# Weight sums of a down-projection made by accumulating DMAs instead of VectorE

## The chip, the core and the metric

The kernel runs on one core of a Trainium2 chip. The metric is the device time of one execution in microseconds (us); the kernel before takes 1341.7 us (median of three runs, 1338.76 to 1344.27). The core's engines work at the same time, each through its own list of instructions in order, and wait for one another by semaphores: TensorE (PE) does the matmuls, VectorE (DVE) and ScalarE (ACT) the elementwise work, GpSimd (POOL) small things, and SyncE (SP) issues nearly all transfers (DMAs). A DMA issued from any of them is carried out by the core's 16 DMA engines.

## The reference, cut to what matters

Two decoder layers over 512 positions of width 1024. Each layer has a token mixer (attention beside a gated delta rule) and then a channel mixer, in which the change lies:

```python
def conv_glu_ffn(h, ffn_w_in, ffn_conv_w, ffn_conv_b, ffn_w_out):
    u = causal_dwconv(h @ ffn_w_in, ffn_conv_w) + ffn_conv_b
    gate, up = jnp.split(u, 2, axis=-1)
    return (jax.nn.gelu(gate, approximate=True) * up) @ ffn_w_out
...
for l in range(DEPTH):              # DEPTH = 2
    ...
    h = rms_norm(x, norm_pre_ffn[l])
    f = conv_glu_ffn(h, ffn_w_in[l], ffn_conv_w[l], ffn_conv_b[l], ffn_w_out[l])
    x = x + rms_norm(f, norm_post_ffn[l]).astype(x.dtype)
```

`ffn_w_in` is 1024 x 5632, `ffn_w_out` (the down-projection) 2816 x 1024, all float32.

## The kernel before, in words

**Precision.** Each float32 operand of a large matmul is split into a high part, rounded by ACT to the PE's format (`wh`, `hh`), and a remainder, formed by DVE (`wl`, `hl`); a product is three matmuls (`three`).

**Up-projection** (`chan_proj`, called with `glu`). The 5632 columns are taken 128 at a time: 44 *weight tiles* of 1024 x 128 (512 KB), each giving 24 matmuls of 512 columns. Each tile goes through `load_w`: an SP load into `st` (three buffers), ACT's cast into `wh` (three buffers), DVE's remainder into `wl` (three). A load therefore waits on SP until DVE has finished with the tile three back, and a cast waits until PE has finished with the tile three back. The first four tiles (`early`) are done in two halves and kept in other buffers. Tiles alternate: a gate tile and an up tile make one *block* `jb` of 128 hidden channels, so there are 22 blocks of two tiles. After each tile `glu` applies the convolution (ACT, then two DVE operations, `fgu`) and after the second one the GELU and the product, which is `hid[jb]` (`g`).

**Down-projection** (`products`). It is a 2 x 2 block product done with seven multiplications instead of eight. The weight is cut in four quarters, W00, W01, W10, W11 (first index: half of the 2816 rows; second: half of the 1024 columns). Three products use quarters as they are; four use sums: U1 = W00 + W01, T3 = W01 + W11, T2 = W00 + T3, T4 = W10 + T2. Each quarter has 11 pieces of 128 rows.

**The sums** (`weight_sums`, line 855). They are made during the up-projection, a piece `k` at a time. At the blocks listed in `SUMS_AT` (line 32) the four 128 x 512 pieces of 256 KB are loaded into `ws` buffers. At the next block `sums.pop(0)()` (line 893) runs `add`: four in-place additions on DVE, in an order in which the second overwrites an operand of the first, the third reads the first's result and overwrites an operand of the second, and the fourth reads the third's result. Then SP stores the four results into DRAM tensors (`wsum`; the profile drops digits, so U1 is `U` there, and T2, T3 and T4 are `T`), from which `products` loads them much later.

**What sets the order.** A scheduler places the instructions of each engine by the priorities given in `prio` and by its own estimate of durations; once placed, the order on an engine is fixed. SP in particular works through one list: a store whose data is not ready holds up every load behind it.

Of the kernel before, what the change touches and what calls it, by code (L numbers as in the profile page):

```python
# [13 lines left out]
OP = mybir.AluOpType  # L14
# [14 lines left out]
NF = 22  # L29
EPS = 1e-6  # L30
NB = 32
SUMS_AT = (0, 2, 3, 5, 7, 8, 10, 12, 13, 15, 17)


class Engines:
# [51 lines left out]
def hybrid_trunk(ctx: ExitStack, tc: tile.TileContext, a, out):  # L87
    nc = Engines(tc)
# [43 lines left out]
    def big(name, dtype=F32, shape=(P, T), tag="b2", bufs=None):  # L132
        return bp.tile(list(shape), dtype, name=name, tag=tag, bufs=bufs)
# [7 lines left out]
    def pair(name, shape=(P, 2, T)):  # L141
        return big(name, F32, shape, "b4", 2)
# [202 lines left out]
    for l in range(NL):  # L345
# [500 lines left out]
        hid, accs, xf = [], {}, {}  # L846
# [3 lines left out]
        def w_f2(kh, s, k, n=1):  # L850
            return a["w_f2"][l, kh, s][:, k:k + n, :]

        sums = []

        def weight_sums(k):

            w = {}
            for kh in range(2):
                for s in range(2):
                    w[kh, s] = big("ws")  # L860
                    nc.sync.dma_start(w[kh, s].unsqueeze(1), w_f2(kh, s, k))

            def add():
                for o, i in (((1, 1), (0, 1)), ((0, 1), (0, 0)), ((0, 0), (1, 1)), ((1, 0), (0, 0))):
                    nc.vector.tensor_tensor(w[o], w[o], w[i], op=OP.add)
                for v, o in zip(wsum, ((0, 1), (1, 1), (0, 0), (1, 0))):
                    nc.sync.dma_start(v[:, k, :], w[o])

            sums.append(add)

        def operand(p, k, src):
            xf[p, k] = big("xf", F32R, (P, 2, T // 2))
            split(xf[p, k][:, 0, :], xf[p, k][:, 1, :], src)
# [3 lines left out]
        def glu(b, ps):  # L877
            jb, g = b // 2, b % 2
            cb = jb + g * NF
            if g == 0:  # L880
                accs[jb] = pair("fgu")
            acc = accs[jb][:, g, :]
            nc.scalar.activation(acc, ps, AF.Identity, scale=fw[:, l, cb, 2:3], bias=fb[:, l, cb:cb + 1])
            for j in range(1, 3):
                nc.vector.scalar_tensor_tensor(acc[:, j:], ps[:, :T - j], fw[:, l, cb, 2 - j:3 - j], acc[:, j:],
                                               op0=OP.mult, op1=OP.add)
            if g == 1:
                ga = accs[jb][:, 0, :]
                nc.scalar.activation(ga, ga, AF.Gelu_apprx_tanh)
                hid.append(big("g"))  # L890
                nc.vector.tensor_tensor(hid[jb], ga, acc, op=OP.mult)
                if sums:
                    sums.pop(0)()
                if jb in SUMS_AT:
                    weight_sums(SUMS_AT.index(jb))
                if jb >= half:
                    k = jb - half
                    x1, x2 = hid[k], hid[jb]
                    operand("X11", k, x1[:, r1])
                    nc.vector.tensor_tensor(x1[:, r1], x1[:, r1], x1[:, r2], op=OP.subtract)  # L900
                    nc.vector.tensor_tensor(x1[:, r2], x1[:, r2], x2[:, r2], op=OP.subtract)
                    operand("D", k, x1[:, r2])

        with prio(L + 7):
            run(chan_proj(lambda b: a["w_f1"][l, b // 2 + NF * (b % 2)], 2 * NF, 4, glu, turns))
# [185 lines left out]
```

## Time and profile before

| | |
|---|---|
| time, median of 3 | 1341.7 us (1338.76 to 1344.27) |
| profiled execution, its own time | 1343.61 us |
| its span, first to last instruction | 1341.7 us |
| PE busy | 1304.3 us (97%) |
| DVE busy | 1009.1 us (75%) |
| ACT busy | 725.3 us (54%) |
| POOL busy | 187.3 us (14%) |
| the additions on DVE (`ws<-ws`), both layers | 60.7 us, 88 operations |
| moved by DMA | 193.14 MB, mean 144 GB/s |

The up-projection of the first layer runs from about 333 to 566 us of the span, that of the second from about 994 to 1228 us. In the rows of a timeline or of the chain of waits the first column is the start and the second the length, in us; in rows of groups "x44" is a count, followed by busy time and mean ns of one, and after the second bar by the idle time of the engine just before them and what ended it; in a table by stretches each engine has busy us and its number of instructions, then come the clock that TensorE was granted, the mean busy share of the 16 DMA engines, and the rate. "PE pm" is a matmul into one of the large accumulators.

### The profile page before, as it was taken

Reading aid. Unit: us, or ns where it says so; the run is one execution under the profiler, and the core shown is the slowest. Engines: PE = TensorE matmul, PEld = TensorE weight load, DVE = VectorE, ACT = ScalarE, POOL = GpSimd, SP = SyncE. Lnnn points to the kernel's source line nnn. Section 1 sums busy time; section 2 is a strip of 40 time slices with the busy share of each in tenths; the row PEclk is TensorE's granted clock in tenths of the full one; section 3 lists DMA queues with packets and bytes.
Section 4 is the critical chain, followed back from the end, with each engine's and each line's share of the span. In section 5 each row is a group of like instructions: output and inputs, shape, how many; then the busy total and the mean of one; then the engine's idle time right before and its main releaser. Section 6 shows DMA issues by size and latency. Waiting matters only on the chain.

```text
span 1341.7 us, 19369 instructions
## 1 busy us (share of the span) xinstructions
PE 1304.3 (97%) x6892; PEld 1083.4 (81%) x6892; DVE 1009.1 (75%) x1956; ACT 725.3 (54%) x1458; POOL 187.3 (14%) x246
## 2 busy tenths in 40 slices
PE   8999999999999999999999999998999999999997
PEld 6787877878888888888777877877888888888876
DVE  6656888868576788798777568888667767888885
ACT  5635966665333444467546369666543334444673
POOL 0019421111000000030010293102010000001201
PEclk9999999999999999999999999999999999999999
DMA  6233211243466566366642422104335566653665
GB/s 227 92 106 95 71 53 36 82 144 131 136 230 219 188 219 212 110 179 185 218 164 72 124 82 73 52 19 134 118 126 188 191 224 198 222 187 105 201 184 162
DMA packets 75489, 193.14 MB, mean 144 GB/s; under 512 B 13409, under 2 KB 13953, under 8 KB 75394
## 3 DMA queue, kind: packets, MB, share of 16 engines
q1 hardware_dynamic: 74882, 190.87, 44.4%
q0 software_dynamic: 512, 1.05, 0.4%
q8 instruction: 54, 0.88, 0.3%
q14 instruction: 41, 0.34, 0.1%
HBM read 161.99 MB, written 29.90 MB: 143 GB/s over the span
## 4 chain that ended last, share of the span: by engine, by line
PE 80%; DVE 8%; ACT 6%; POOL 2%; DMA 2%; issue 2%; SPq 0%; POOLq 0%; DVEq 0%; ACTq 0%
PE pm L54 67%; PE pw L54 13%; DVE wl L54 2%; ACT junk L54 1%; DVE xs L54 1%; ACT wh L54 1%; DVE x L54 1%; ACT sc L54 1%; POOL nr L54 1%; DVE hl L54 1%; DVE xf L54 1%; DMA st<-in_w_f 1%; ACT Vt L54 0%; POOL pr L54 0%; POOL qs L54 0%
## 5 line engine op out<-in xcount | busy, mean ns | idle before, releaser
L54 DVE TENSOR_TENSOR wl<-st,wh 128x1024 fp32r<-128x1024 f32 (+1 forms) x250 | 282.7, 1136 | 163.1 <-ACT wh L54 161.0
L54 PE MATMUL pm<-hh,wh 128*128 128x512 f32 (+1 forms) x1024 | 373.6, 367 | 3.9 <-ACT hh L54 3.9
L54 ACT ACTIVATE wh<-st 128x1024 fp32r<-128x1024 f32 (+1 forms) x254 | 245.8, 972 | 242.3 <-PE pm L54 223.4
L54 PE MATMUL pm<-hl,wh 128*128 128x512 f32 (+1 forms) x1024 | 375.2, 368 | 0.0
L54 PE MATMUL pm<-hh,wl 128*128 128x512 f32 (+1 forms) x1024 | 374.0, 367 | 1.1 <-DVE wl L54 1.1
L54 PEld LDWEIGHTS pm<-hh,wh 128*128 128x128 f32 x1024 | 194.8, 191 | 34.6 <-ACT hh L54 5.2
L54 PEld LDWEIGHTS pm<-hh,wl 128*128 128x128 f32 x1024 | 195.1, 191 | 30.4 <-DVE wl L54 1.3
L54 PEld LDWEIGHTS pm<-hl,wh 128*128 128x128 f32 x1024 | 195.3, 192 | 29.0
L54 PE MATMUL pm<-wh,xf 128*128 128x512 f32 x528 | 164.5, 391 | 0.0
L54 PE MATMUL pm<-wh,hh 128*128 128x512 f32 x384 | 154.4, 405 | 0.0
L54 PE MATMUL pm<-wh,hl 128*128 128x512 f32 x384 | 153.1, 399 | 0.0
L54 PE MATMUL pm<-wl,hh 128*128 128x512 f32 x384 | 151.2, 395 | 0.8 <-DVE wl L54 0.8
L54 DVE SCALAR_TENSOR_TENSOR fgu<-pm,fw,fgu 128x511 f32<-128x511 f32 (+1 forms) x176 | 131.1, 745 | 21.9 <-ACT fgu L54 19.9
L54 PEld LDWEIGHTS pm<-wh,xf 128*128 128x128 f32 x528 | 99.1, 188 | 21.2 <-ACT e L54 0.6
L54 PE MATMUL pm<-wl,xf 128*128 128x512 f32 x264 | 103.6, 392 | 0.5 <-DVE wl L54 0.5
L54 POOL TENSOR_TENSOR g<-g 128x256 f32<-128x256 f32 x22 | 25.4, 1174 | 493.1 <-DVE xf L54 493.1
L54 PEld LDWEIGHTS pm<-wl,hh 128*128 128x128 f32 x384 | 72.4, 189 | 14.8 <-DVE wl L54 2.0
L54 PEld LDWEIGHTS pm<-wh,hl 128*128 128x128 f32 x384 | 72.4, 188 | 14.2
L54 PEld LDWEIGHTS pm<-wh,hh 128*128 128x128 f32 x384 | 72.1, 189 | 14.0 <-ACT wh L54 0.5
L54 ACT ACTIVATE sc<-sc,mx 128x128 f32<-128x128 f32 (+3 forms) x128 | 69.5, 558 | 22.2 <-DVE mx L54 21.6
L54 ACT ACTIVATE fgu<-pm,fb,fw 128x512 f32<-128x512 f32 x88 | 66.9, 761 | 18.6 <-PE pm L54 18.6
L54 ACT ACTIVATE fgu<-fgu 128x512 f32<-128x512 f32 x44 | 27.8, 632 | 90.8 <-DVE fgu L54 90.7
(228 smaller groups left out, 1801.5 us busy)
## 6 DMA issues: line engine op xcount, KB each, us to landing
st<-in_w_f SPq DMA_DIRECT2D x118, 512.0 KB, 3.7
ws<-in_w_f SPq DMA_DIRECT2D x88, 256.0 KB, 4.7
T<-ws SPq DMA_DIRECT2D x66, 256.0 KB, 2.3
st<-in_w_at SPq DMA_DIRECT2D x32, 512.0 KB, 3.7
st<-T SPq DMA_DIRECT2D x30, 512.0 KB, 4.0
st<-in_w_dn SPq DMA_DIRECT2D x24, 512.0 KB, 3.8
st<-in_w_out SPq DMA_DIRECT2D x16, 512.0 KB, 3.6
U<-ws SPq DMA_DIRECT2D x22, 256.0 KB, 2.0
```

The source lines that it names most:

```text
L54: r = f(*args, **kwargs)
```

## The change

The four additions are no longer DVE operations. Each is a DMA issued from POOL that reads one `ws` buffer and accumulates into another, both in SBUF (`accum_op=OP.add`). The stores stay on SP, but are put one block after the additions: a list of (block, action) replaces the list of actions. Two entries of `SUMS_AT` move, 3 to 4 and 12 to 11, so that in the order of blocks the pieces come alone at 0 and 2, in neighbouring pairs at (4, 5), (7, 8), (10, 11), and alone at 13, 15, 17. A store now waits for an accumulating DMA where it waited for DVE.

```diff
-SUMS_AT = (0, 2, 3, 5, 7, 8, 10, 12, 13, 15, 17)
+SUMS_AT = (0, 2, 4, 5, 7, 8, 10, 11, 13, 15, 17)
...
             def add():
                 for o, i in (((1, 1), (0, 1)), ((0, 1), (0, 0)), ((0, 0), (1, 1)), ((1, 0), (0, 0))):
-                    nc.vector.tensor_tensor(w[o], w[o], w[i], op=OP.add)
+                    nc.gpsimd.dma_start(w[o], w[i], accum_op=OP.add)
+
+            def store():
                 for v, o in zip(wsum, ((0, 1), (1, 1), (0, 0), (1, 0))):
                     nc.sync.dma_start(v[:, k, :], w[o])
 
-            sums.append(add)
+            sums.append((len(hid), add))
+            sums.append((len(hid) + 1, store))
...
-                if sums:
-                    sums.pop(0)()
+                while sums and sums[0][0] < len(hid):
+                    sums.pop(0)[1]()
```

On SP, from the first pieces of the first layer on, the list of transfers was this (`st<-in_w_f` loads a weight tile, `ws<-in_w_f` the four pieces; T_3578 is T3, U_3577 is U1, T_3579 is T2, T_3580 is T4):

```order
L54 DMA st<-in_w_f 128x1024 x10
L54 DMA ws<-in_w_f 128x512 x4
L54 DMA T_3578<-ws 128x512
L54 DMA U_3577<-ws 128x512
L54 DMA T_3579<-ws 128x512
L54 DMA T_3580<-ws 128x512
L54 DMA st<-in_w_f 128x1024 x2
L54 DMA ws<-in_w_f 128x512 x4
```

In the changed kernel, at the same place for a pair of pieces (blocks 4 and 5), it is this:

```order
L54 DMA ws<-in_w_f 128x512 x4
L54 DMA st<-in_w_f 128x1024
L54 DMA T_3578<-ws 128x512
L54 DMA st<-in_w_f 128x1024
L54 DMA ws<-in_w_f 128x512 x4
L54 DMA U_3577<-ws 128x512
L54 DMA T_3579<-ws 128x512
L54 DMA st<-in_w_f 128x1024
L54 DMA T_3580<-ws 128x512
L54 DMA T_3578<-ws 128x512
L54 DMA st<-in_w_f 128x1024
L54 DMA U_3577<-ws 128x512
```

The four stores of a piece, which stood together, are now spread, with loads of weight tiles (and of the next pieces) queued behind each of them. For a lone piece the list is the pieces' load, a tile, T3, a tile, U1 and T2, a tile, T4, a tile, and then the next pieces' load.

On POOL, with the semaphores each waits for, the accumulating DMAs of the first two pieces of the first layer stand like this (DMASW0 to DMASW7 are the semaphores of the DMAs that POOL issues, DMAHW those of SP's):

```order
L54 DMA ws<-ws 128x512 [waits DMAHW7_49,DMAHW5_49,PE_49]
L54 DMA ws<-ws 128x512 [waits DMAHW4_49,DMASW0_49]
L54 DMA ws<-ws 128x512 [waits DMASW1_49,PE_49]
L54 DMA ws<-ws 128x512 [waits DMAHW6_49,DMASW2_49]
L54 DMA ws<-ws 128x512 [waits DMAHW7_49,DMAHW1_49,PE_49]
L54 DMA ws<-ws 128x512 [waits DMAHW6_49,DMASW4_49]
L54 DMA ws<-ws 128x512 [waits DMASW5_49]
```

POOL had nothing at this place before. Now 44 DMAs per layer stand there, and the second, third and fourth of each piece wait for the one ahead of them; the first of a piece waits for its loads alone.

## The prediction

> **What bounds the kernel now.** I first read the chain of waits through the up-projection, where every changed instruction lies. For the two layers it is one piece each (start, length):
>
> ```profile
> 332.56 278.21 PE pm L54 x1289
> 994.40 278.22 PE pm L54 x1289
> ```
>
> For 278 us TensorE never waits for anything. The table by stretches, over the 44 weight tiles alone, says the same: PE is busy in all of its 233.4 us at full clock, POOL does nothing, and the DMA engines are busy 58% of the time.
>
> ```profile
> 332.60:566.00 233.40, 233.40 (x1093) 195.98 (x1092) 169.06 (x243) 92.54 (x127) 0.00 (x0) 1.00 0.58 191
> ```
>
> So DVE, at 169 of 233 us, sets nothing here. The pace is ACT's evacuation of one tile after another (`fgu<-pm`), which PE releases; the two rows of `wh` are casts of later tiles:
>
> ```profile
> 365.40 0.76 ACT L54 ACTIVATE fgu<-pm,fb,fw 128x512 f32<-128x512 f32 x1
> ...
> 369.87 1.06 ACT L54 ACTIVATE wh<-st 128x1024 fp32r<-128x1024 f32 x1 [0.95 <-PE pm L54]
> 370.84 0.76 ACT L54 ACTIVATE fgu<-pm,fb,fw 128x512 f32<-128x512 f32 x1
> ```
>
> 370.84 - 365.40 = 5.44 us for a tile, 10.9 us for a block of two.
>
> What else could stop PE is SP's list. It is read in time order, together with DVE's addition:
>
> ```profile
> 298.09 35.21 SPq L54 DMA_DIRECT2D st<-in_w_f  x10
> 333.35 1.86 SPq L54 DMA_DIRECT2D ws<-in_w_f  x4
> 352.08 0.33 SPq L54 DMA_DIRECT2D T<-ws  x1
> ...
> 355.90 5.77 SPq L54 DMA_DIRECT2D st<-in_w_f  x2
> 361.71 2.46 SPq L54 DMA_DIRECT2D ws<-in_w_f  x4
> ```
> ```profile
> 368.73 2.87 DVE L54 TENSOR_TENSOR ws<-ws 128x512 f32<-128x512 f32 x4 [0.54 <-DMA ws<-in_w_f]
> 371.52 1.22 DVE L54 TENSOR_TENSOR wl<-st,wh 128x1024 fp32r<-128x1024 f32 x1
> ```
>
> Already now SP stands still at a store for 17 us (335.2 to 352.1), and PE doesn't notice. How long may it? The eleventh tile (ten were loaded ahead) is issued at 355.90. PE needs it when ten tiles are through, and this row of groups, over 339 to 382 us, counts ten evacuations, of which the last is the row behind it:
>
> ```profile
> L54 ACT ACTIVATE fgu<-pm,fb,fw 128x512 f32<-128x512 f32 x10 | 7.7, 765 | 9.3 <-PE pm L54 9.3
> ```
> ```profile
> 381.72 0.76 ACT L54 ACTIVATE fgu<-pm,fb,fw 128x512 f32<-128x512 f32 x1
> ```
>
> Before 381.7 come the load (3.7 us to landing, the row below), the cast 1.06 and the remainder 1.22, with some 0.2 between: 6.2 us. So a tile's load may be late by 381.7 - 6.2 - 355.9 = **19.6 us** before PE waits.
>
> ```profile
> st<-in_w_f SPq DMA_DIRECT2D x118, 512.0 KB, 3.7
> ws<-in_w_f SPq DMA_DIRECT2D x88, 256.0 KB, 4.7
> ```
>
> **The change, part by part.** *Removed:* 44 additions per layer from DVE, 60.7 us in both:
>
> ```profile
> L54 DVE TENSOR_TENSOR ws<-ws 128x512 f32<-128x512 f32 x88 | 60.7, 689 | 8.4 <-DMA ws<-in_w_f 6.4
> ```
>
> Worth on the path: nothing, since no PE instruction there waited for DVE. In the whole program the waits of matmuls and of weight loads for `wl` are
>
> ```profile
> PE pm L54 <- DVE wl L54: 2.3, 5, 1.1
> PEld pm L54 <- DVE wl L54: 5.7, 12, 1.3
> ```
>
> 8.0 us, which is the most that a freer DVE could give back; since the two chains above hold none of them, I take 0. The order of ACT's and DVE's other work also shifts a little at the same spots; 169 - 44 x 0.69 = 139 us of DVE work hides under 233 us of PE, so 0 as well.
>
> *Added:* 88 accumulating DMAs from POOL. POOL has nothing else there (it sat idle for 244 us before its next operation, which comes after the last tile), so its issue time costs nothing by itself:
>
> ```profile
> 574.45 2.61 POOL L54 TENSOR_TENSOR g<-g 128x256 f32<-128x256 f32 x3 [244.12 <-DVE xf L54]
> ```
>
> What costs is that in each piece's four DMAs each waits for the one ahead, and that SP's stores, with tile loads behind them, wait for those. Call L the time from the issue of one accumulating DMA to that of the next one that waits for it. The trace has no accumulating DMA. Its nearest row is a 64 KB copy that POOL issues, with the POOL operation that waits for it:
>
> ```profile
> 189.33 0.57 POOL L54 DMA_DIRECT2D zc<-dX  x1 [3.07 <-PE pw L54]
> 191.59 1.53 POOL L54 COPY zt<-zc 32x128 f32<-32x128 f32 x2 [1.69 <-DMA zc<-dX]
> ```
>
> 191.59 - 189.33 = 2.26 us. That is the lower bound of L (a quarter of the bytes, nothing added). The upper bound is the longest landing of any of these 256 KB transfers, 6.9 us:
>
> ```profile
> DMA to landing us min/median/max: 2.0/3.6/6.9
> ```
>
> Between them: all 16 engines at work move 191 / 0.58 = 329 GB/s, so 256 KB take 0.80 us and 64 KB 0.20. An accumulation reads both its source and its destination, two passes: L = 2.26 - 0.20 + 2 x 0.80 = 3.66 us with free engines. They aren't always free: SP issues a tile (512 KB, 1.6 us of all engines) right behind T3's and T2's stores, that is, as the second and the fourth DMA begin; at worst each costs a full 1.6, which is +0.8 on the mean, so 4.5. I take 3.9, nearer the free end, because a tile's load begins some time after its issue and overlaps only partly.
>
> The Trainium skill, "DMA: Bandwidth & Descriptors", section "Anatomy of one DMA — SWDGE (gpsimd) path", puts a POOL-issued DMA at 2.0 us plus its bytes at 436 GB/s. For 64 KB that is 2.15 against the measured 2.26; for two passes of 256 KB it gives an estimated 3.2 instead of my 3.66 to 4.5. By it the margin below would be 0.9 us, not 0.2; I keep the rate of this stage's own row.
>
> *Moved, and the tipping point.* A lone piece must get through SP in 2 blocks, 21.8 us. From the last of its four loads (issued at 361.71 + 2.46 - 0.37 = 363.8) to the first addition (368.73) are 4.9 us; then four links; then T4's store, a tile and the four loads of the next piece, 0.3 + 0.4 + 1.9 = 2.6: together 7.5 + 4L. A pair has 3 blocks, 32.6 us, and the second piece's chain begins when POOL has issued the first's fourth DMA (0.6 us): 4.9 + 3L + 0.6 + 4L + 2.6 = 8.1 + 7L. Between blocks 2 and 17 lie three lone pieces and three pairs, so the lateness that builds up in a layer is 3 (4L - 14.3) + 3 (7L - 24.5) = 33L - 116 us. The first 19.6 are free: PE loses 33L - 136 per layer, **66L - 272** in both, from L = 4.1 us on. At 3.9 the lateness is 13 us a layer, hidden under the tiles loaded ahead: 0.
>
> *Traffic.* In 233.4 us the engines are busy 0.58 x 233.4 = 135; 44 accumulations of two passes add 44 x 1.6 = 70, together 205 of 233: it fits.
>
> Sum: 0 - 0 + 0 on the profiled execution's 1343.6 us (span 1341.7, and 1.9 around it). The median of the runs shown is 1.9 us below that execution, so I predict 1342 for the median.
>
> **The rivals.**
>
> *The chain paces SP (slower).* If L is over 4.1 us, stores hold the tile loads back until PE starves, at each of the later pieces. For it: the margin is 0.2 us on a price that no row shows, and each further 0.1 us costs 6.6. Against it: only L decides, and 3.66 is what free engines give. At L = 4.8 it costs 66 x 4.8 - 272 = 45: 1387 us; at the upper bound of 6.9, 183: 1525.
>
> *The DMA engines are full.* If an accumulation takes three passes (two reads and a write apart), 44 x 2.4 = 106, and 135 + 106 = 241 us of work in 233: +8 a layer, some 1357 us. Against it: copies read and write in one pass at the rate above.
>
> *POOL is held up while it issues.* POOL's issue may be slowed by DVE. At worst each waits for one DVE operation of 1.22 us: L = 3.9 + 1.2 = 5.1, 66 x 5.1 - 272 = 65, 1407 us. The issue row above took 0.57 with DVE busy in the same slices, which speaks against it. The Trainium skill, "SBUF — State Buffer", section "Who interferes with whom", has such a rule: DMAs issued by GpSimd can be starved by DVE operations that take the port pair both share. It names copies and tensor_scalar, not the two-input operations that fill this stage; no row here shows such a stall.
>
> *A freer DVE helps after all.* All 8.0 us of waits for `wl` vanish: 1334. Against it: they lie outside the stage.
>
> **How the numbers follow.** What a measurement can tell from no change is about 0.5%, 6.7 us. No change, 1342 us: 0.55. The chain paces SP: 0.32. Engines full: 0.06. POOL held up: 0.03. Faster: 0.04. So faster 0.04, same 0.55, slower 0.41. Alone, the no-change case would range from 1337 to 1348. For 8 in 10 I go up to L = 4.9 (66 x 4.9 - 272 = 51, 1393), which leaves about a third of the chain rival and half of POOL's above, some 0.14, and down to 1336, which leaves 0.03: 1336 to 1395.
>
> **What would show it.** Right: the chain of waits still has one piece of about 278 us per layer, evacuations 5.44 us apart, starts of dependent `ws<-ws` DMAs on POOL 3.6 to 4.1 us apart, and SP's waits now on `ws<-ws` DMAs instead of DVE's. Wrong: PE waits for `wl` or for `st` behind ACT in the second half of the up-projection, evacuations more than 5.44 us apart there, dependent DMAs over 4.1 us apart (the chain), or a DMA share near 1 (full engines), or POOL's issues much over 0.57 us (held up). If L is under 4 and PE starves all the same, my account of SP's list is wrong.

## The result, and the profile after

The changed kernel takes **1446.8 us** (median of three runs, 1443.03 to 1450.1) against 1341.7 before: 1.0776 times as long, 95% interval 1.0753 to 1.08. Some 105 us are lost, about 50 in each layer's up-projection. The forecast was 1342, with a range up to 1395; what happened is its rival "the chain paces SP", at more than twice the 45 us that it gave for L = 4.8.

The profiled execution has a span of 1440.9 us, 99.2 more than before. These are rows of its page: totals, the queue of POOL's DMAs, the chain of waits by line, and issues with median us to landing:

```profile
PE 1340.2 (93%) x6892; PEld 1091.6 (76%) x6892; DVE 956.8 (66%) x1868; ACT 723.2 (50%) x1458; POOL 263.6 (18%) x334
...
q0 software_dynamic: 13184, 24.12, 9.5%
...
PE pm L54 42%; DMA ws<-ws 15%; PE pw L54 12%; DMA ws<-in_w_f 4%; DVE wl L54 2%; SPq L54 2%; ACT junk L54 1%; DMA st<-in_w_f 1%; ACT wh L54 1%; DVE xs L54 1%; DVE xf L54 1%; DVE x L54 1%; POOL nr L54 1%; ACT sc L54 1%; POOL ws L54 1%
...
ws<-ws POOLq DMA_DIRECT2D x88, 256.0 KB, 5.0
```

VectorE is freed as meant (956.8 us busy, 1009.1 before), but 15% of the chain of waits is now the accumulating DMAs themselves. Where before one piece of 278 us stood in this chain, PE's own work now ends after 97 us, and from there the chain goes from link to link (start, length, us):

```profile
330.39 97.36 PE pm L54 x491
428.31 5.33 DMA ws<-ws
435.98 5.02 DMA ws<-in_w_f
445.09 6.59 DMA ws<-ws
```

The table by stretches shows the same: untouched to 405 us, then PE is busy in 184 of 214 us, at a lower clock, while the DMA engines, at 0.74, are not full.

```profile
332.60:405.00 72.40, 72.40 (x374) 62.25 (x373) 37.01 (x45) 25.86 (x32) 8.68 (x10) 1.00 0.66 178
405.00:619.00 214.00, 184.12 (x726) 142.58 (x724) 104.93 (x152) 67.31 (x96) 29.31 (x34) 0.94 0.74 200
```

Who waits for whom, in the whole program (total us, times, longest): SP waits for the accumulating DMAs, where before (first row) it waited for VectorE's sums.

```profile
SPq L54 <- DVE ws L54: 65.1, 77, 12.4
```
```profile
SPq L54 <- DMA ws<-ws: 327.2, 81, 6.6
```

So ACT waits for weight tiles, and PE for ACT's casts.

```profile
ACT wh L54 <- DMA st<-in_w_f: 207.7, 55, 6.5
...
PEld pm L54 <- ACT wh L54: 57.9, 28, 4.8
...
PE pm L54 <- ACT wh L54: 46.8, 22, 4.4
```

Now the links. POOL's timeline shows one pair of pieces and the start of the next:

```profile
396.08 0.86 POOL L54 DMA_DIRECT2D ws<-ws  x1 [13.57 <-ACT wh L54]
399.64 0.86 POOL L54 DMA_DIRECT2D ws<-ws  x1 [2.70 <-DMA ws<-ws]
406.53 0.86 POOL L54 DMA_DIRECT2D ws<-ws  x1 [6.03 <-DMA ws<-ws]
410.97 1.75 POOL L54 DMA_DIRECT2D ws<-ws  x2 [3.58 <-DMA ws<-ws]
418.57 0.86 POOL L54 DMA_DIRECT2D ws<-ws  x1 [5.86 <-issue]
424.40 0.86 POOL L54 DMA_DIRECT2D ws<-ws  x1 [4.97 <-DMA ws<-ws]
428.31 0.86 POOL L54 DMA_DIRECT2D ws<-ws  x1 [3.04 <-PE pm L54]
441.56 0.86 POOL L54 DMA_DIRECT2D ws<-ws  x1 [12.39 <-DMA ws<-in_w_f]
```

The row of 410.97 holds two issues, the first piece's fourth and, at 411.50, the second piece's first. From start to start the links take 3.56, 6.89, 4.44, then 7.07 (from 411.50), 5.83, 3.91 us, and the next pair begins 45.5 us after this one, where PE's pace allows 32.6. Two sizes stand side by side: 3.6 to 4.4 us, and 5.8 to 7.1. What tells them apart is what SP issues at that moment. Here, for the piece before, are SP's rows and then POOL's:

```profile
371.58 0.33 SPq L54 DMA_DIRECT2D T<-ws  x1
372.00 0.38 SPq L54 DMA_DIRECT2D st<-in_w_f  x1
377.59 0.33 SPq L54 DMA_DIRECT2D U<-ws  x1
```
```profile
368.29 0.85 POOL L54 DMA_DIRECT2D ws<-ws  x1 [17.81 <-PE pm L54]
371.85 0.86 POOL L54 DMA_DIRECT2D ws<-ws  x1 [2.71 <-DMA ws<-ws]
377.86 0.86 POOL L54 DMA_DIRECT2D ws<-ws  x1 [5.15 <-DMA ws<-ws]
```

The first link is free: 371.85 - 368.29 = 3.56 us. Its landing lets SP issue T3's store (371.58) and then, at 372.00, the weight tile that stood behind it, 0.15 us after POOL issues the second accumulation (371.85). The packets in the trace's DMA records, in the order in which they ran, are:

```
us               queue  packets of        one takes
372.4  - 373.3   SP     2048 B (store)    0.09 us
373.1  - 375.95  SP     4096 B (tile)     0.16 us for most, 0.7 to 1.2 for twelve of 128
375.65 - 377.2   POOL   2048 B (accum.)   0.18 us
```

The accumulation's own packets take 1.5 us, as in a free link, but none moves before the first engines are through with their part of the tile (375.64): 377.86 - 371.85 = 6.01 us. The second and the fourth link of nearly every piece are built like this, since SP puts a tile behind T3's and T2's stores; so is the first link of a pair's second piece, which is issued right behind the first piece's fourth.

The Trainium skill, "DMA: Bandwidth & Descriptors", section "Queues, rings and completion order", says that each DMA engine takes turns between queues, but empties a whole packet of some 9 to 17 descriptors of one before it turns to the next. A tile is 8 rows for each of 16 engines, so that its share would fit into one such packet. The trace agrees in time: its records don't name the engine, but the accumulation's packets begin (375.65) as the first shares of the tile end (375.64).

### The profile page after: what moved, and what is told of

It is laid out like the page before. It is cut to its first block, busy times and chain, and to the rows that moved or that the text cites. A ratio compares the mean times of both kernels' runs of the same rounds, so it can differ in the third digit from the quotient of the medians.

```text
span 1440.9 us, 19486 instructions
## 1 busy us (share of the span) xinstructions
PE 1340.2 (93%) x6892; PEld 1091.6 (76%) x6892; DVE 956.8 (66%) x1868; ACT 723.2 (50%) x1458; POOL 263.6 (18%) x334
## 4 chain that ended last, share of the span: by engine, by line
PE 54%; DMA 21%; DVE 9%; issue 6%; ACT 5%; POOL 3%; SPq 2%; POOLq 0%; DVEq 0%; ACTq 0%
PE pm L54 42%; DMA ws<-ws 15%; PE pw L54 12%; DMA ws<-in_w_f 4%; DVE wl L54 2%; SPq L54 2%; ACT junk L54 1%; DMA st<-in_w_f 1%; ACT wh L54 1%; DVE xs L54 1%; DVE xf L54 1%; DVE x L54 1%; POOL nr L54 1%; ACT sc L54 1%; POOL ws L54 1%
## 5 line engine op out<-in xcount | busy, mean ns | idle before, releaser
L54 PE MATMUL pm<-hh,wh 128*128 128x512 f32 (+1 forms) x1024 | 382.3, 376 | 43.7 <-ACT wh L54 39.4
L54 PE MATMUL pm<-hh,wl 128*128 128x512 f32 (+1 forms) x1024 | 382.3, 375 | 9.5 <-DVE wl L54 9.2
L54 PE MATMUL pm<-hl,wh 128*128 128x512 f32 (+1 forms) x1024 | 380.7, 373 | 0.0
L54 PEld LDWEIGHTS pm<-hl,wh 128*128 128x128 f32 x1024 | 198.2, 194 | 30.2
L54 PE MATMUL pm<-wh,xf 128*128 128x512 f32 x528 | 169.3, 399 | 7.4 <-ACT wh L54 7.4
L54 POOL DMA_DIRECT2D ws<-ws x88 | 76.0, 886 | 468.6 <-DMA ws<-ws 221.6
L54 PE MATMUL pm<-wl,xf 128*128 128x512 f32 x264 | 106.7, 404 | 8.0 <-DVE wl L54 8.0
L54 ACT ACTIVATE xf<-g 128x256 fp32r<-128x256 f32 x154 | 59.6, 410 | 39.8 <-PE pm L54 18.9
L54 DVE TENSOR_TENSOR xf<-g,xf 128x256 fp32r<-128x256 f32 x154 | 66.2, 454 | 20.0 <-ACT xf L54 19.7
```

The costliest lines, as they stand in the source:

```text
L54: r = f(*args, **kwargs)
```

## The experiments

All are edits of the changed kernel.

**1. Additions back on VectorE, all else as changed.**

```diff
-                    nc.gpsimd.dma_start(w[o], w[i], accum_op=OP.add)
+                    nc.vector.tensor_tensor(w[o], w[o], w[i], op=OP.add)
```

> The four additions are DVE operations again; the stores stay one block later and the block list stays the new one. If the accumulating DMAs are the cause, the loss goes: 1342 us, within 7. If the new block list or the later place of the stores is the cause, it stays near 1447.

Measured: 1342.98 us, 1.0004 times before (0.9993 to 1.0016). The new block list and the stores one block later cost nothing.

**2. The same accumulating DMAs, none waiting for another.** Each adds a constant tile of the same size.

```diff
-                    nc.gpsimd.dma_start(w[o], w[i], accum_op=OP.add)
+                    nc.gpsimd.dma_start(w[o], rope.rearrange("p a t d -> p (a t d)"), accum_op=OP.add)
```

> The same 88 accumulating DMAs of the same size, but each adds a constant tile instead of another piece, so none waits for the one ahead (the sums, and so the output, are left out). Chain theory (SP's stores wait for a chain of four): the four land within some 8 us of the first one's issue, a lone piece takes 4.9 + 8 + 2.6 = 15.5 of its 21.8 us, and PE doesn't wait: 1342, within 7. Traffic theory (the accumulations fill the DMA engines, wherever they stand): near 1447.

Measured: 1342.98 us, 1.001 times before (0.9999 to 1.002). The chain of waits has its long piece again, and in the up-projection PE is never idle with the DMA engines at 0.85, more than in the change:

```profile
332.58 278.22 PE pm L54 x1289
```
```profile
332.60:566.00 233.40, 233.40 (x1093) 195.95 (x1093) 142.25 (x199) 92.39 (x127) 38.60 (x44) 1.00 0.85 240
```

The traffic of 88 accumulations and POOL's issues cost nothing; the loss is in the order in which they must follow one another.

**3. The same chain of plain copies.**

```diff
-                    nc.gpsimd.dma_start(w[o], w[i], accum_op=OP.add)
+                    nc.gpsimd.dma_start(w[o], w[i])
```

> The same chain of 88 DMAs from POOL, but each copies instead of adding (the sums, and so the output, are left out). A free link should fall from 3.56 us to about 2.75, since 8 packets of 85 ns take the place of 8 of 188. Theory that a DMA of the chain waits behind a whole tile load: the links with a tile load ahead keep their extra 2.5 to 3.3 us (5.3 to 6 us), and the time stays well above 1342, at 1355 to 1385. Theory that the adding is the price: all links near 2.75 and 1342.

Measured: 1376.5 us (one run). The first three of POOL's rows for one piece:

```profile
532.58 0.54 POOL L54 DMA_DIRECT2D ws<-ws  x1 [12.44 <-DMA ws<-in_w_f]
535.22 0.54 POOL L54 DMA_DIRECT2D ws<-ws  x1 [2.11 <-DMA ws<-ws]
539.32 0.54 POOL L54 DMA_DIRECT2D ws<-ws  x1 [3.56 <-DMA ws<-ws]
```

Free links are 2.64 us instead of 3.56; behind a tile they are 4.1 here and up to 6.2 elsewhere. The adding itself is 0.9 us of a link; even without it the chain still holds SP, and costs a third of the loss.

**4. The four stores issued from POOL.** SP then has nothing to wait for in the chain.

```diff
-                    nc.sync.dma_start(v[:, k, :], w[o])
+                    nc.gpsimd.dma_start(v[:, k, :], w[o])
```

> The accumulating chain is kept, but its results are stored by POOL, so that SP never waits for it. Theory that SP's list is what carries the loss: the up-projection is one unbroken piece on PE again, and only the down-projection may wait a little for late sums: 1342 to 1365. Theory that traffic or POOL is the cause: still above 1420.

Measured: 1392.2 us, 1.0414 (1.0347 to 1.0481). I had expected at most 1365, and missed. PE now runs unbroken for 168 us instead of 97, and up to the 40th tile the loads come 19.6 us before PE needs them, as before the change. So SP's hold is indeed gone; what stops PE then is ACT, which waits for a buffer that the chain still has (`xf`, the operands of the down-projection, comes from the same 41 buffers as `ws`):

```profile
330.60 167.84 PE pm L54 x802
```
```profile
ACT xf L54 <- DMA ws<-ws: 18.7, 2, 9.4
ACT xf L54 <- DMA U<-ws: 16.9, 1, 16.9
```

The last two rows are of 500 to 600 us. Here the pieces' first links follow one another 16 to 27 us apart (22 on the mean), one chain at a time, where PE's pace asks for 18 (15 blocks of 10.88 us for 9 pieces), and pieces that are loaded but not yet summed fill the buffers. One wait had been hiding another.

**5. Two chains at once.** Pieces are loaded in pairs, and the links of the two alternate on POOL; their stores alternate too, and stay on SP.

```diff
-SUMS_AT = (0, 2, 4, 5, 7, 8, 10, 11, 13, 15, 17)
+SUMS_AT = (0, 0, 3, 3, 7, 7, 10, 10, 13, 13, 17)
...
-                    nc.gpsimd.dma_start(w[o], w[i], accum_op=OP.add)
+                    for _, w in both:
+                        nc.gpsimd.dma_start(w[o], w[i], accum_op=OP.add)
```

> The sums stay accumulating DMAs in chains of four, stored by SP, with the same bytes; but two pieces are loaded at the same block and their chains run at once on POOL (blocks 0, 3, 7, 10, 13 with two pieces, 17 with one), so that two pieces take about five links instead of eight. Chain theory: 5 + 5 x 5 + 4 = 34 us for two pieces of the 33 to 44 us that PE gives them, within the slack of 20: 1342 to 1352. If the accumulating DMAs can't overlap, so that only their number counts: 1420 to 1450.

Measured: 1369.7 us, 1.0216 (1.0183 to 1.0248): three quarters of the loss are back. I had expected all of it (1342 to 1352), and missed. SP still stands behind some 24 us of links in a row, and tiles come late in places; from 333 to 640 us ACT waits for them so:

```profile
ACT wh L54 <- DMA st<-in_w_f: 39.4, 8, 7.1
```

**6. Only two of the four sums as DMAs** (T2 and T4; T3 and U1 on VectorE).

```diff
-                    nc.gpsimd.dma_start(w[o], w[i], accum_op=OP.add)
+                    if o[0] == 1 and i[0] == 0 and o[1] == 0 or o == (0, 0):
+                        nc.gpsimd.dma_start(w[o], w[i], accum_op=OP.add)
+                    else:
+                        nc.vector.tensor_tensor(w[o], w[o], w[i], op=OP.add)
```

> T3 and U1 are made by DVE again, T2 and T4 by accumulating DMAs: a chain of two links. Chain theory: a lone piece takes 7.5 + 2 x 5 = 17.5 of 21.8 us and a pair about 8.1 + 4 x 5 = 28 of 32.6, nothing builds up: 1342, within 7. If every accumulating DMA costs its share: half of the loss, 1390 to 1400.

Measured: 1341.4 us, 0.9998 (0.9986 to 1.0011). Two links fit into a piece's time, four don't.

**7. The old block list with everything else changed.** `SUMS_AT` as before the change.

> The changed kernel with the block list of before (0, 2, 3, 5, 7, 8, 10, 12, 13, 15, 17). It too has three neighbouring pairs and otherwise lone pieces, so the chain theory gives the same loss: 1437 to 1457. If the moved entries matter, over 1465 or under 1425.

Measured: 1437.8 us (one run). With the old list nearly the whole loss is there too, so the moved entries are not its cause.

**8. Half of each weight tile's load** (from the fifth tile on, half is loaded and used twice).

```diff
-                w = load_w(w_src(b), [KC, P], None, eng(b))
+                w = load_w(w_src(b)[:, :KC // 2, :], [KC // 2, P], None, eng(b)) if nblk == 2 * NF else load_w(w_src(b), [KC, P], None, eng(b))
```

> From the fifth weight tile on, SP loads only half of each up-projection tile (256 KB), which is used twice (the other half of the weight, and so the output, is left out); sums, chains and stores as in the change. Theory that a link waits until the tile load ahead of it has gone through the engines: the links behind a tile fall from 6.1 to about 4.8 us and the time to 1360 to 1395. Theory of a fixed price per link under load: links and time as before, near 1447.

Measured: 1396.7 us (one run), 2 us above the range. The edit halves a tile's own load, cast and remainder too, so the time alone would not single out the links; their lengths do. The links behind a tile are 4.9 us (and up to 5.9) where they were 6 to 7, the free ones still 3.5, with no accumulation changed:

```profile
519.28 0.86 POOL L54 DMA_DIRECT2D ws<-ws  x1 [10.99 <-DMA ws<-in_w_f]
522.82 0.86 POOL L54 DMA_DIRECT2D ws<-ws  x1 [2.68 <-DMA ws<-ws]
527.68 0.86 POOL L54 DMA_DIRECT2D ws<-ws  x1 [4.01 <-DMA ws<-ws]
```

So what makes a link long is the load in front of it, and about half of the loss goes with half of the load.

**9. Both: two chains at once, and the stores from POOL** (edits 4 and 5 together).

> Two chains at once (as in the run with pairs at one block) and the stores issued on POOL's queue (as in the run with the stores there): the first edit alone left 1369.7 us because SP stood behind the chain for longer than the tiles' slack in places, the second alone left 1392.2 because one chain at a time could not keep the pieces' pace and the buffers of the quarters filled up. Together neither is left: SP waits for no chain, and a pair of chains takes about 5 links of 5 us = 25 us of the 33 us from pair to pair. If these two waits are all that the change costs: 1342, at most 1350. If accumulating DMAs beside tile loads cost by themselves once the stores are on POOL: near 1390 as with the stores alone on POOL. If only SP's part goes and buffers still fill: 1350 to 1370.

Measured: 1343.8 us, 1.0018 (1.0008 to 1.0028). All 88 accumulations are there, each waits for the one it depends on, and PE runs through again, with the DMA engines at 0.84:

```profile
329.97 278.22 PE pm L54 x1289
```
```profile
332.60:566.00 233.40, 233.40 (x1083) 195.49 (x1082) 142.65 (x198) 93.23 (x127) 63.00 (x88) 1.00 0.84 238
```

This is the run that closes the account: the chained accumulations cost nothing by themselves, and the two waits behind them (SP's list, and the pace of one chain at a time) all but some 2 of the 105 us. VectorE does 142.65 us of work here instead of 169.06, and nothing comes of it, since PE sets the pace. No version beat the kernel before.

**10 to 12. The end of a layer.** Lateness by the prediction's own formula, with the links as measured, gives two thirds of the loss (below). My first idea for the rest was the last piece's own chain, behind which the down-projection's first loads stand on SP. Three runs take it away in different ways: its sums on VectorE, its stores on POOL, its sums left out.

```diff
+                    if k == half - 1:
+                        nc.vector.tensor_tensor(w[o], w[o], w[i], op=OP.add)
+                    else:
+                        nc.gpsimd.dma_start(w[o], w[i], accum_op=OP.add)
```

> Only the eleventh piece's sums are made by VectorE again; the ten others are chained as in the change. Account under test: of the 53 us that a layer's up-projection loses, the lateness that builds up between the second and the last piece is 56 us less the 19.6 that the tiles loaded ahead cover, some 37; the other 16 come from the last piece's own chain, behind which the last weight tile and the down-projection's first loads stand on SP. By it, 2 x 16 = 32 us come back: 1446.8 - 32 = 1415, between 1408 and 1422. If the lateness is all and the last piece adds nothing: 1440 to 1450. If the lateness counts less than this and the last piece is most of it: under 1400.

Measured: 1447.1 us, 1.078 (1.0762 to 1.0798): nothing gained. VectorE now stands at the late loads of this piece, with tiles' remainders behind it, for one of which PE then waits 10.6 us:

```profile
590.38 1.42 DVE L54 TENSOR_TENSOR ws<-ws 128x512 f32<-128x512 f32 x2 [15.44 <-DMA ws<-in_w_f]
```

```diff
-                    nc.sync.dma_start(v[:, k, :], w[o])
+                    (nc.sync if k < half - 1 else nc.gpsimd).dma_start(v[:, k, :], w[o])
```

> Only the four stores of the eleventh piece are issued from POOL instead of SP; its sums stay chained DMAs like all others. With the eleventh piece's sums on VectorE the time did not move (1447.1), but there VectorE itself stood 15 us at the first of these additions, with the remainders of two weight tiles behind it, so that run does not settle it. Here nothing stands in SP's list behind the last piece's loads: the last two weight tiles can be loaded as soon as their buffers are free, from about 583 us on, so that the last evacuation comes near 583 + 6.2 + 3 x 5.44 = 605.5 instead of 617.9. If the last piece's own chain costs as much as this: 12 us in each layer, 1446.8 - 25 = 1422, between 1412 and 1430. If the lateness before it is all: 1440 to 1450.

Measured: 1437.6 us, 1.0705 (1.0679 to 1.073). SP is free, and ACT stands instead, for a buffer as in experiment 4:

```profile
599.83 0.42 ACT L54 ACTIVATE xf<-g 128x256 fp32r<-128x256 f32 x1 [9.64 <-DMA ws<-ws]
```

```diff
+                    if k < half - 1:
+                        nc.gpsimd.dma_start(w[o], w[i], accum_op=OP.add)
```

> The eleventh piece's sums are left out (its quarters are stored as they were loaded); the ten others are chained as in the change. With its stores moved to POOL the time fell by 9 us only (1437.6), since ScalarE then stood 9.6 us at a buffer that the last chain still held; with its sums on VectorE not at all, since VectorE then stood at the piece's loads. Here the last piece has no chain, no held buffer and no addition: the last weight tiles follow at once (from about 583 us on), PE has three tiles left from about 587, and the last evacuation comes near 587 + 3 x 5.44 = 603 to 606 instead of 617.9. If the end of a layer waits for the last piece's chain, by whichever engine: 12 to 15 us per layer, 1446.8 - 27 = 1420, between 1414 and 1426. If the lateness built up before it is all: over 1437.

Measured: 1436.9 us, 1.0697 (1.0666 to 1.0728). With no last chain at all, 10 us come back, not the 27 that I had worked out. My idea falls for the larger part.

What the rows show instead is ACT's fixed order. A tile's cast stands on ACT directly ahead of the evacuation of the tile three before it. While PE sets the pace, the two fall together; when the load is late, finished tiles wait behind a cast that can't begin. Here is one such place in the middle of the stage:

```profile
432.44 1.06 ACT L54 ACTIVATE wh<-st 128x1024 fp32r<-128x1024 f32 x1 [5.23 <-DMA st<-in_w_f]
433.41 0.77 ACT L54 ACTIVATE fgu<-pm,fb,fw 128x512 f32<-128x512 f32 x1
```

How much this is can be counted. The last weight tile is needed, for PE not to starve, 33 paces of 5.44 us after the tenth evacuation and 6.2 us before that. In the changed kernel this is 379.56 + 179.5 - 6.2 = 552.9; it is issued at 591.33, 38.5 late, and the last evacuation comes at 617.86, from the first (337.51) 280.4 us instead of 227.0:

```profile
337.51 0.78 ACT L54 ACTIVATE fgu<-pm,fb,fw 128x512 f32<-128x512 f32 x1 [6.48 <-PE pm L54]
...
379.56 0.76 ACT L54 ACTIVATE fgu<-pm,fb,fw 128x512 f32<-128x512 f32 x1
...
617.86 0.76 ACT L54 ACTIVATE fgu<-pm,fb,fw 128x512 f32<-128x512 f32 x1
```
```profile
591.33 0.38 SPq L54 DMA_DIRECT2D st<-in_w_f  x1
```

Counted in this way for the runs, both layers:

| | last tile's load, us late | first to last evacuation, us over 227.0 |
|---|---|---|
| before | -19.3, -19.3 | 0, 0 |
| changed | 38.5, 35.6 | 53.4, 49.9 |
| plain copies | 4.8, 7.3 | 16.5, 17.4 |
| half tiles | 15.7, 13.4 | 28.1, 25.9 |
| last piece unsummed | 31.1, 36.8 | 44.2, 50.1 |
| both (experiment 9) | -19.6, -19.6 | 0, 0 |

In each of these runs with late tiles the stage loses the last tile's lateness and 10 to 15 us on top, with or without a last chain. (With the last piece unsummed the tile before the last is the latest, 36.0 and 41.7 us; counted from it, 8 us are on top. Experiments 10 and 11, not in the table, have 16 and 21 us on top of the last tile; in 4 and 5 ACT's buffer waits and earlier tiles count for more than the last one.)

Where most of the top lies can be read in the changed kernel. PE is through with its last tile at 604.4 us, 40.7 later than at PE's pace, which is the late load and 2 us more. But ACT evacuates this tile only at 617.86, 13.5 us later, where before the change it was 0.8 us (565.90 and 566.68):

```profile
604.01 0.39 PE L54 MATMUL pm<-hh,wl 128*128 128x512 f32 x1
```
```profile
611.98 1.06 ACT L54 ACTIVATE wh<-st 128x1024 fp32r<-128x1024 f32 x1 [4.00 <-DMA st<-in_w_f]
```

The second row is the cast of a tile of the down-projection, which stands ahead of the evacuation of the last tile but one; SP issued its load at 607.53, behind the last piece's chain. The same stretch, from PE's last matmul of the stage to its evacuation, is 10.4 us with plain copies, 8.9 with half tiles and 6.8 with the last piece unsummed. In that last run no cast waits for a load any more after 591 us, but ACT and VectorE still have three tiles to work off, one every 4 to 5 us. So the last chain seems to be a part of the top, and the late evacuations on ACT the rest. This is read from rows and times; no run changed ACT's order, so it is not shown by an experiment.

## Why the prediction was wrong

**What bounds the kernel** held: PE's unbroken chain, the pace of 5.44 us, and the margin of a tile's load before PE waits: the prediction's 19.6 us, counted anew for the last tile of before, are 19.3. *Removed* held too: VectorE's 60.7 us were worth nothing (experiments 1, 9).

**Added** is the step that failed. Its price of an accumulating DMA with free engines, L = 3.66 us, was right: free links measure 3.53 to 3.66 us in most places, and up to 4.4 elsewhere. What it put on top was wrong: 0.2 us, 0.8 at worst, for a tile's load beside it, "because a tile's load begins some time after its issue and overlaps only partly". The accumulation doesn't share the engines with that load, it stands behind the whole of it, and in every second link, because the same landing that releases the accumulation releases the load, and the load's packets come first. That adds 2.5 to 3.5 us to such a link. A tile was also priced too low, at 1.6 us of all engines by its bytes: in the records above its packets run for 2.8 us. Over the 27 links between starts of the second to the tenth piece of the first layer (135.8 us) and six last links of some 5.65 us to their landing, L is (135.8 + 33.9) / 33 = 5.14 us where 3.9 was taken. The row that should have warned was quoted there: the longest landing of a 256 KB transfer, 6.9 us, an upper bound that came true in part. POOL's issue, 0.86 us and not 0.57, lies within the 3.56 and adds little.

**Moved, and the tipping point** held in its form. 33L - 116 gives 53.7 us of lateness for L = 5.14. From the second piece's first link to the last piece's, the trace has 587.65 - 368.29 = 219.4 us, where 15 blocks at PE's pace are 163.2: 56.2. Less the free 19.6, some 34 to 37 a layer; the last tile is late by 38.5 and 35.6.

```profile
587.65 0.86 POOL L54 DMA_DIRECT2D ws<-ws  x1 [12.68 <-DMA ws<-in_w_f]
```

**"PE loses 33L - 136"** was too small even so: at L = 5.14 it gives 66 x 5.14 - 272 = 67 us, and 1409. The stage also loses the 10 to 15 us per layer with which a late load comes to the end of the layer, which the prediction didn't have. Both layers together, 74 us of lateness and 29 on top are the 103.3 that the evacuations come late; the span is 99.2 longer. Of the 4 us between them 2.2 are the first layer's first evacuation, which comes earlier than before the change (337.51 and 339.67), and some 2 are regained after the stage.

**The rivals.** "The chain paces SP" was right in place, in mechanism and in its sign (dependent links over 4.1 us apart); its chance, 0.32, was too low, since the margin of 0.2 us was known to rest on a price that no row showed. "DMA engines are full" falls: 0.74 in the change, 0.85 without loss in experiment 2. "POOL is held up" falls: 80 of 88 issues took 0.85 to 0.88 us, two 0.94, and six, each right behind another issue, 1.21; in experiment 2 some took up to 1.9, and it cost nothing. "A freer VectorE helps" falls by experiment 9.

## What to carry to other kernels

When a transfer must follow another, price it with the transfers that the same event releases: here a load queued behind the first one's store started together with it and went ahead of it. Put such a chain's stores on a queue with nothing behind them, and run two chains at once where one can't keep the pace; but first see whether the engine that is relieved sets any pace at all. When a wait is taken away and the time stays, look for the next holder of the same chain (here SP's list, then buffers on ACT, then VectorE's list).

## What the runs showed of the hardware

- A 256 KB accumulating DMA within SBUF, issued from POOL, took 3.53 to 3.66 us from issue to the next link's where little ran beside it, a plain copy 2.5 to 2.8. In the records the accumulation's packets of 2048 B take 0.18 to 0.19 us each, those of plain stores of the same size 0.09; POOL spends 0.85 us on most of its issues, 0.54 on that of a copy.
- Once PE starves for some us, the clock that it is granted falls to half for some time after work has come back. In the changed kernel this followed each of PE's six waits of 2.65 to 4.05 us between 405 and 580 us of the first layer, for 3.4 or 6.8 us. Around the wait of 3.38 us that ends at 479.63, in stretches of 3 us (PE busy, clock, DMA share, rate):

```profile
476.00:479.00 3.00, 0.25 (x2) 1.00 0.81 215
479.00:482.00 3.00, 2.34 (x5) 0.56 0.47 130
482.00:485.00 3.00, 3.00 (x9) 0.50 0.98 348
```

The Trainium skill, "TensorE: Matmul & The Clock Gate", section "HAM oscillation — how this bites in real kernels", describes this for waits on DMAs over 3.4 us. The trace agrees in kind, but four of the six waits lay between 2.65 and 3.08 us. It seems to cost little here: from 405 to 619 us SP waits 139.7 us for accumulations and 0.3 for VectorE's remainders, so loads aren't held by a slower PE, and plain copies lose their 10 to 12 us on top at a mean clock of 1.00 in this stretch. No run took the lower clock away by itself.

```profile
SPq L54 <- DMA ws<-ws: 139.7, 34, 6.6
...
SPq L54 <- DVE wl L54: 0.3, 1, 0.3
```
